# A chain of matmuls and transposes on the output rows, added behind a two-layer block

## The chip, the cores and the metric

The kernel runs on one core of one Trainium2 chip. The time is the device time of one execution in microseconds; before the change its median over two runs is 1359.74 us (1359.56 to 1359.93).

## The reference

The block takes 256 latent tokens and 256 context tokens of 1024 numbers each through two layers and gives back the latent tokens. A layer, cut to what matters:

```python
h = rms_norm(x, norm_w) * (1 + scale) + shift          # scale, shift, gate from c and w_ada
proj = h @ w_in                                        # q, k, v and gate paths of four mixers, merge gates
ys = [windowed, neighbourhood, dense, differential]    # four attentions over latent and context keys
ys = [silu(gate_path) * y for y in ys]
merged = sum(sigmoid(merge_gate[i]) * (ys[i] @ w_br[i]) for i in range(4))
x = x + gate * (merged @ w_out)                        # the second layer's x, latent tokens alone, is the output
```

Everything is float32. What the change adds is in no part of this.

## The kernel before

All weights stream from memory in chunks of 128 x 1024 (`raw`). Each chunk is split exactly into two parts of type fp32r, `wh` and `wl`; so are the activations (`hT`, `yT`, and `gT` and `yT` again for the merged branches). A product is three matmuls, high by high, high by low and low by high (`mm3`), on the full array of 128 rows by 128 columns, with 512, 384 or 256 moving columns. Profiles name the fp32r operands of matmuls `f32`. The one bf16 operand of TensorE is the zero tile of the warm-up: nine matmuls at the start (`WARM`), whose result nobody reads. Transposes are done on TensorE too, 128 x 128 in f32 against the identity `ident`.

The order of the work is not written by hand. The program is recorded first (`Recorder.alt`: each operation with its dependences, found from the parts of the tiles that it reads and writes). Then `schedule` chooses each engine's order by list scheduling: an engine takes the first operation of its list that is ready, TensorE in the order of the recording, the others by the latest start that an earlier schedule gave them (`deadlines`). `search` does this six times, keeps the order whose end by its own model is earliest, and issues that. Matmuls that write one PSUM tile keep their order (`self.chain`). Tiles of one tag share a few slots (`BUFS`: three for `t2k`, two for `t4k`); a tile may be taken ahead of earlier ones of its tag within limits (`RESERVE`, `WINDOW`).

The end of the kernel is `out_proj` of layer 1 (lines 1518 to 1561), with two passes of 512 output columns (`dg`) over two tiles of 128 tokens (`t`). A block's eight times three matmuls fill one PSUM tile; VectorE multiplies it by the gate (`tmp`, tag `t2k`), VectorE or GpSimd adds it to the residual rows `new` (tag `K2`, shown as `K`), and SyncE stores the result to `out`. The very last block, second tile and second pass, goes in two halves of 256 columns. `new[:, 1]` is the second tile of 128 tokens, all 1024 columns; its last quarter is the last thing computed.

In the profile nearly every instruction stands on line 270, the helper that issues the recorded operations; so tiles tell them apart, not lines.

Of the kernel before, what the change touches and what calls it, by code (L numbers as in the profile page):

```python
# [36 lines left out]
# the grid's tokens go column by column, so that 128 of them are half of the grid. Mixer B's keys: one half, the  # L37
# context, the other half; a half's windows reach 8 columns into the other one
# [5 lines left out]
# token-major groups: blocks of 128 columns (mixer, q/k/v/g, index);  # L44
# "S?" is a mixer's gate path and "G??" a merge gate, both feature-major.
# [34 lines left out]
# the adaLN units computed after a group: the next layer's scale and shift, this layer's gate  # L80
# [9 lines left out]
# ---- instruction order: the program is recorded first, then each engine's order is chosen by list  # L90
# scheduling against a model of the engines, and issued in that order ----
ADA = "DPDDGDDGPGGDDGDD"                       # layer 0, shift and scale: units on VectorE (D), GpSimd (G), TensorE (P)
# [8 lines left out]
GATE = 4096 / 1200.0                         # TensorE runs at half its clock after such a time with little work  # L101
# from the end of an instruction to the start of one that needs it; for TensorE with some margin, so that what it
# has in hand covers a late operand
# [10 lines left out]
def _extent(ap):  # L114
    """(partition range, range of elements within a partition's row) that an access pattern touches"""
    dims = ap.ap
    row = dims[0][0]
    n = dims[0][1]
    off = ap.offset
    if row <= 0:  # L120
        return None
    if ap.space == DRAM:
        return 0, 1, min([off] + [off + s * (c - 1) for s, c in dims if s < 0]), 1 + off + sum(
            s * (c - 1) for s, c in dims if s > 0)
    p0, f0 = divmod(off, row)
    lo = hi = f0
    for s, c in dims[1:]:
        if s < 0:
            lo += s * (c - 1)
        else:  # L130
            hi += s * (c - 1)
    return p0, p0 + n, lo, hi + 1


def _run(ap):
    """elements of the contiguous pieces"""
    return ap.ap[-1][1] if ap.ap[-1][0] == 1 else 1
# [13 lines left out]
# PSUM banks are shared by the three uses, each of which is sure of some  # L151
# [22 lines left out]
class Recorder:  # L174
    def __init__(self, nc, pools, plan=None):
# [3 lines left out]
        if plan is not None:                     # tiles are allocated in the order in which the plan uses them  # L179
            self.made = {}  # L180
            for k, slot in plan.slots:
                self.made[k] = self.make(plan.spec[k], slot)
# [3 lines left out]
        self.acc = {}                            # tile name -> [(op, write, extent)]  # L186
        self.tag = {}                            # tile name -> (tag, bufs)
        self.stream = set()                      # tiles of the weights' stream, loaded in order
        self.chain = {}                          # PSUM tile -> its last matmul
# [10 lines left out]
    def tile(self, *spec):  # L200
        """a tile as (pool, shape, type, tag, number of the tag's slots); the plan gives it one of the slots"""
# [13 lines left out]
    # operations that more than one engine can do; the schedule chooses  # L215
# [11 lines left out]
    def alt(self, ways):  # L227
        """one operation, as {engine: (method, args, kw)}"""
# [30 lines left out]
        if "tensor" in ways:                     # accumulation groups of one bank must not interleave  # L259
# [38 lines left out]
    def schedule(self):  # L298
# [6 lines left out]
        # slots: a tile may overtake earlier ones of its tag while a slot is left for those  # L305
# [16 lines left out]
        bank = {}                                # PSUM tile -> {engine: end of its last access}  # L322
        avail = {e: [] for e in ENGS}            # (prio, i) of ops whose producers are all scheduled

        def slot_time(o):
            """time from which the op's tiles have slots, or None"""
# [119 lines left out]
    def deadlines(self):  # L446
        """from a schedule: the latest start of each op at which no instruction of TensorE is late"""
# [20 lines left out]
    def search(self, tries):  # L468
        """the best of several schedules, each with priorities from the deadlines of the one before"""
# [26 lines left out]
class _Builder:  # L496
# [106 lines left out]
    def expand_bias(self, l):  # L603
        """rpbx[h, t, q, i, j] = rpb[h, i + 4, (24 t + j) - (32 t + q) + 15]: column q of half t of the grid,
        rows i of the table that a grid of 4 rows reaches, the 40 columns of keys that the half's windows
        reach; entries outside of a window hold other table entries and are masked later.
        rpbq[h, t, 4 q + r] = rpbx[h, t, q, 3 - r:7 - r]: row r of the grid"""
# [9 lines left out]
    def silu_c(self):  # L617
        """twice silu(c) and silu(c_ctx): as columns, and as rows in every partition"""
# [108 lines left out]
    def split_ops(self, i):  # L727
        """closures that split chunk i, in two halves"""
# [16 lines left out]
    def raw_chunk(self, *key):  # L745
        """the next chunk as it comes"""
# [6 lines left out]
    def chunk(self, *key):  # L753
        """the next chunk, split"""
# [14 lines left out]
    def mm3(self, out, sh, sl, mh, ml, first, last):  # L769
        """stationary (sh + sl) times moving (mh + ml)"""  # L770
# [34 lines left out]
    def ada_unit_pool(self, l, u):  # L805
        """the same on GpSimd, sums on ScalarE"""
# [9 lines left out]
    def ada_unit_pe(self, l, u):  # L816
        """the same on TensorE, as rows that are then transposed"""
# [26 lines left out]
    def norm(self, xt, n):  # L844
        """rows of n token tiles, normalised"""
# [11 lines left out]
    def modulate(self, l, kts, cols, srcs):  # L857
        """h = xn * scale + shift for k tiles kts; srcs: (v, source AP [128, kts, tokens], columns in hf)"""
# [30 lines left out]
    def project_first(self, pre):  # L889
        """the first two groups, chunk by chunk, while h is computed"""  # L890
# [42 lines left out]
    def project_T(self, n, *key):  # L933
        """one block of 128 columns, feature-major"""
# [11 lines left out]
    def sel(self, tab, blocks):  # L946
        """[128, blocks, 64] from a table [128, 2 or 4 mixers, q/k, 64]"""
# [7 lines left out]
    def tabs(self, blocks, t, w):  # L955
        """rotary table w (0 cos, 1 swapped sin) times gain"""
# [5 lines left out]
    def evac_unit(self, u, ps, t, c0, nh):  # L962
        """square sums and raw copy of nh heads of tile t"""
# [12 lines left out]
    def prep_steps(self, u, ts):  # L976
        """norm, gain and rotary of unit u on tiles ts, in place"""
# [34 lines left out]
    def make_q(self, u, blk, tiles):  # L1012
        """[128, 2, tokens]: head 0 as (hi; lo), head 1 as (lo; hi)"""
# [10 lines left out]
    def make_k(self, u, blk):  # L1024
        """[128, hi/lo, 2, 512]: each head's keys in both halves of the partitions"""
# [11 lines left out]
    def evac_v(self, v, ps, t, c0, diff):  # L1037
        """diff: [hi | lo] of 128 columns; else per head [hi | lo] of 64"""
# [10 lines left out]
    def evac_diff_gate(self, g, ps, t):  # L1049
        """token-major gate of mixer D: 2 silu(gate) * subln gain * (1 - lam_init)"""  # L1050
# [13 lines left out]
    def next_bias(self, l, h):  # L1064
        """the bias of head h, loaded one head ahead"""
# [8 lines left out]
    def score_x(self, mix, h, q, j, k, kj, bias, qt, nm):  # L1074
# [9 lines left out]
        elif mix == MIX_B:  # L1084
            near = 32 if qt == 0 else 8          # columns of the grid in front of the context's keys
# [21 lines left out]
    def expo_x(self, S, nm, s, cs=slice(0, 512)):  # L1107
        """numerators, in columns cs of a tile, and their sum"""
# [190 lines left out]
    def split_tiles(self, tag, n):  # L1299
        """room for both parts of [128, n]: one tile if they fit in it"""  # L1300
# [130 lines left out]
    def silu_group(self, l, name):  # L1431
# [3 lines left out]
        per = 512 // n                           # blocks of a tile  # L1435
# [13 lines left out]
    def gate_logits(self, l, m, pr):  # L1449
        """two blocks of 128 output channels of one branch: gate logits"""  # L1450
# [12 lines left out]
    def gate_merge(self, l, m, pr):  # L1463
        """the same blocks: branch projection, gate, merge"""
# [33 lines left out]
    def store_gates(self, l):  # L1498
        """the gate's columns as rows in memory"""
# [9 lines left out]
    def load_gates(self, l, v):  # L1509
        """the gate in every partition: [128 (any token), 1024]"""  # L1510
# [7 lines left out]
    def out_proj(self, l, v, mT, src, finish):  # L1518
# [14 lines left out]
        for dg in range(2):  # L1533
            # (tokens, columns, sum); the last block in halves: one is finished while the other is computed
# [50 lines left out]
    def build(self):  # L1585
# [27 lines left out]
        for l in range(DEPTH):  # L1613
# [41 lines left out]
            else:  # L1655
                self.out_proj(l, 0, mT, self.xmid, a["out"])


class _Unit:
    """up to two blocks of 128 q/k columns of one mixer, over the token tiles"""  # L1660

    def __init__(self, blocks):
# [3 lines left out]
        self.ready = 0                           # tiles whose q/k are prepared  # L1666


def _rows(w):
    """[K, N] -> [K/256, 128, 2 * N]: rows in chunks of 256"""  # L1670
# [3 lines left out]
def _blocks(w, nb):  # L1674
    """[K, N] -> [N / (128 nb), 128, nb * K]: columns in nb blocks of 128, all rows"""
# [5 lines left out]
def _tokens():  # L1681
    """where in the sequence the tokens come from"""
# [4 lines left out]
def _shape_constants():  # L1687
# [6 lines left out]
    # indexed by where the factor comes from: what lands in half 0 is negated  # L1694
# [61 lines left out]
```

## Time and profile before

| | |
|---|---|
| median of the two runs | 1359.74 us (1359.56 to 1359.93) |
| span of the profiled execution | 1355.9 us; its own time is given as this span alone |
| what lies around the span, against the median | 3.8 us |
| TensorE (PE) busy | 1266.3 us, 93% of the span, 7286 matmuls |
| VectorE (DVE) busy | 1094.4 us, 81% |
| ScalarE (ACT), GpSimd (POOL) busy | 741.8 us (55%), 696.1 us (51%) |
| mean granted TensorE clock | 0.981 of 2.4 GHz |

The span runs from the first to the last instruction of one execution; the time of a run is a little longer. A matmul is shown with the time from its start to its end, and the next starts before that end; the pace of a row of matmuls is therefore read from their starts, not from their durations. PEld is the loading of the stationary operand, which goes on beside the matmuls. The granted clock is 1.00 at 2.4 GHz and 0.50 at 1.2 GHz.

### The profile page before, as it was taken

Reading aid. Unit: us, or ns where it says so; the run is one execution under the profiler, and the core shown is the slowest. Engines: PE = TensorE matmul, PEld = TensorE weight load, DVE = VectorE, ACT = ScalarE, POOL = GpSimd, SP = SyncE. Lnnn points to the kernel's source line nnn. Section 1 sums busy time; section 2 is a strip of 40 time slices with the busy share of each in tenths; the row PEclk is TensorE's granted clock in tenths of the full one; section 3 lists DMA queues with packets and bytes.
Section 4 is the critical chain, followed back from the end, with each engine's and each line's share of the span. In section 5 each row is a group of like instructions: output and inputs, shape, how many; then the busy total and the mean of one; then the engine's idle time right before and its main releaser. Section 6 shows DMA issues by size and latency. Waiting matters only on the chain. (4 is left out here: it accounts for less than half of the span.)

```text
span 1355.9 us, 21375 instructions
## 1 busy us (share of the span) xinstructions
PE 1266.3 (93%) x7286; PEld 1086.5 (80%) x7286; DVE 1094.4 (81%) x2108; ACT 741.8 (55%) x1738; POOL 696.1 (51%) x694
## 2 busy tenths in 40 slices
PE   7688999999999999999999999899999899899998
PEld 5466778789877989778777887888889899788897
DVE  7999974974998688995788568798995878886877
ACT  6466843463765346633456345577664556554563
POOL 4784224424554655534364236665754756475643
PEclk8899999999999999999999999999999999999999
DMA  6531133313322432243322266231436534343454
GB/s 244 179 123 42 47 105 98 124 58 114 90 87 94 147 114 72 88 153 100 105 63 78 85 208 203 81 125 51 138 114 176 166 121 140 100 127 105 143 168 172
DMA packets 64576, 160.90 MB, mean 119 GB/s; under 512 B 13482, under 2 KB 24914, under 8 KB 64468
## 3 DMA queue, kind: packets, MB, share of 16 engines
q1 hardware_dynamic: 64468, 159.55, 37.3%
q8 instruction: 57, 0.93, 0.3%
q14 instruction: 51, 0.42, 0.1%
HBM read 157.42 MB, written 5.88 MB: 120 GB/s over the span
## 5 line engine op out<-in xcount | busy, mean ns | idle before, releaser
L270 POOL TENSOR_TENSOR wl<-raw,wh 128x512 fp32r<-128x512 f32 (+2 forms) x233 | 307.6, 1324 | 341.0 <-PE ppj L270 179.6
L270 PE MATMUL ppj<-wh,hT 128*128 128x512 f32 (+2 forms) x1424 | 388.2, 351 | 18.5 <-DVE hT L270 14.2
L270 ACT ACTIVATE wh<-raw 128x512 fp32r<-128x512 f32 (+2 forms) x394 | 233.3, 600 | 250.7 <-PE ppj L270 187.9
L270 PE MATMUL ppj<-hT,wh 128*128 128x512 f32 (+1 forms) x1408 | 368.5, 345 | 0.0
L270 PEld LDWEIGHTS ppj<-wh,hT 128*128 128x128 f32 x1424 | 253.5, 192 | 45.1 <-DVE hT L270 16.8
L270 PEld LDWEIGHTS ppj<-hT,wh 128*128 128x128 f32 x1408 | 244.0, 191 | 27.4 <-ACT t2k L270 0.2
L270 DVE TENSOR_TENSOR wl<-raw,wh 128x512 fp32r<-128x512 f32 (+2 forms) x247 | 199.5, 817 | 77.9 <-PE ppj L270 63.3
L270 PE MATMUL ppj<-wl,hT 128*128 128x512 f32 (+2 forms) x712 | 248.3, 349 | 1.2 <-DVE wl L270 0.7
L270 PE MATMUL ppj<-hT,wl 128*128 128x512 f32 (+1 forms) x704 | 242.9, 345 | 1.8 <-DVE wl L270 1.8
L270 PEld LDWEIGHTS ppj<-wl,hT 128*128 128x128 f32 x712 | 136.8, 192 | 14.8 <-POOL wl L270 1.6
L270 ACT ACTIVATE P<-psc,st 128x512 f32<-128x512 f32 (+2 forms) x192 | 114.8, 601 | 60.8 <-DVE st L270 53.3
L270 PEld LDWEIGHTS ppj<-hT,wl 128*128 128x128 f32 x704 | 134.4, 191 | 16.0 <-DVE wl L270 2.5
L270 PE MATMUL ppj<-yT,wh 128*128 128x512 f32 (+1 forms) x512 | 131.7, 341 | 0.4 <-DVE yT L270 0.4
L270 PE MATMUL psc<-K,Q 128*128 128x512 f32 (+2 forms) x384 | 99.1, 367 | 13.8 <-DVE Q L270 8.4
L270 PE MATMUL ptr<-ident,P 128*128 128x128 f32 x560 | 88.1, 277 | 17.4 <-DVE P L270 12.5
L270 DVE TENSOR_REDUCE st<-psc 128x1 f32<-128x512 f32 (+2 forms) x160 | 102.3, 660 | 1.0
L270 POOL TENSOR_TENSOR st<-st,expo 128x8 f32<-128x8 f32 (+3 forms) x68 | 97.5, 1437 | 2.5
L270 PEld LDWEIGHTS ppj<-yT,wh 128*128 128x128 f32 x512 | 87.5, 189 | 10.6 <-DVE yT L270 0.8
L270 PEld LDWEIGHTS ptr<-ident,P 128*128 128x128 f32 x560 | 64.9, 141 | 37.6 <-DVE P L270 10.3
L270 PEld LDWEIGHTS psc<-K,Q 128*128 128x128 f32 x384 | 63.6, 192 | 33.2 <-DVE Q L270 12.0
L270 PE MATMUL ptr<-t4k,V 128*128 128x256 f32 x480 | 78.4, 289 | 11.1 <-DVE t4k L270 9.0
L270 PE MATMUL ppj<-yT,wl 128*128 128x512 f32 (+1 forms) x256 | 86.8, 339 | 1.0 <-DVE wl L270 1.0
(176 smaller groups left out, 2139.2 us busy)
## 6 DMA issues: line engine op xcount, KB each, us to landing
raw<-in_w_G SPq DMA_DIRECT2D x64, 512.0 KB
raw<-in_w_ada SPq DMA_DIRECT2D x43, 512.0 KB
raw<-in_w_br SPq DMA_DIRECT2D x32, 512.0 KB
raw<-in_w_in_D SPq DMA_DIRECT2D x32, 512.0 KB
raw<-in_w_S SPq DMA_DIRECT2D x24, 512.0 KB
raw<-in_w_in_B SPq DMA_DIRECT2D x32, 384.0 KB
raw<-in_w_out SPq DMA_DIRECT2D x24, 512.0 KB
raw<-in_w_in_A SPq DMA_DIRECT2D x8, 512.0 KB
```

The lines of the kernel that those rows point to most:

```text
L270: getattr(getattr(self.nc, eng), fn)(*args, **kw)
```

## The change

`out_proj` of the last layer hands its rows back, and a new method, `strokes`, records work on the second tile of them. VectorE makes four copies: `z` (1024 columns, fp32r), `b` (1024 columns, bf16), `y` (512 columns, f32) and `one` (the identity, fp32r). On these, TensorE does 124 matmuls and transposes, each a group by itself (`start` and `stop` set), into four PSUM tiles that nothing reads:

- 12 fp32r and 12 bf16 matmuls of 512 columns on all 128 rows, and 8 fp32r ones whose columns come in two pieces of 256;
- 12 fp32r and 12 bf16 ones of 128 columns;
- 20 fp32r ones of 512 columns on 64 rows, in turn on the lower and the upper half of the partitions and into two PSUM tiles, then 8 on the lower half alone;
- 6 times such a pair and two matmuls on all rows;
- 8 f32 transposes of 128 x 128, and 8 in fp32r.

The stationary operand has 128 columns in all of them. `LO` and `HI` are partitions 0 to 63 and 64 to 127. Apart from this the diff takes comments and docstrings away.

```diff
             else:
-                self.out_proj(l, 0, mT, self.xmid, a["out"])
+                new = self.out_proj(l, 0, mT, self.xmid, a["out"])
+                self.strokes(new)
...
+    def strokes(self, new):
+        nc = self.nc
+        z = self.t([128, 2, 512], "t4k", F32R)
+        nc.vector.tensor_copy(z.rearrange("p a b -> p (a b)"), new[:, 1])
+        b = self.t([128, 2, 512], "t2k", BF16)
+        nc.vector.tensor_copy(b.rearrange("p a b -> p (a b)"), new[:, 1])
+        y = self.t([128, 512], "t2k")
+        nc.vector.tensor_copy(y, new[:, 1, 0:512])
+        one = self.t([128, 128], "t2k", F32R)
+        nc.vector.tensor_copy(one, self.ident)
+        ps = [self.pt([128, 512], "pj") for _ in range(4)]
+        mm = lambda o, w, x: nc.tensor.matmul(o, w, x, start=True, stop=True)
+        for _ in range(12):
+            mm(ps[0], z[:, 0, 0:128], z[:, 1])
+        for _ in range(12):
+            mm(ps[1], b[:, 0, 0:128], b[:, 1])
+        for _ in range(8):
+            mm(ps[2], z[:, 0, 0:128], z[:, :, 0:256])
+        for _ in range(12):
+            mm(ps[3][:, 0:128], z[:, 0, 0:128], z[:, 1, 0:128])
+        for _ in range(12):
+            mm(ps[0][:, 0:128], b[:, 0, 0:128], b[:, 1, 0:128])
+        for _ in range(10):
+            for h, q in ((0, LO), (1, HI)):
+                mm(ps[1 + h], z[q, 0, 0:128], z[q, 1])
+        for _ in range(8):
+            mm(ps[0], z[LO, 0, 0:128], z[LO, 1])
+        for _ in range(6):
+            for h, q in ((0, LO), (1, HI)):
+                mm(ps[1 + h], z[q, 0, 0:128], z[q, 1])
+            for k in (0, 3):
+                mm(ps[k], z[:, 0, 0:128], z[:, 1])
+        for k in range(8):
+            c = slice(k % 4 * 128, k % 4 * 128 + 128)
+            nc.tensor.transpose(ps[0][:, c], y[:, c], self.ident)
+        for k in range(8):
+            c = slice(k % 4 * 128, k % 4 * 128 + 128)
+            nc.tensor.transpose(ps[1][:, c].bitcast(F32R), z[:, 0, c], one)
```

## Rows read from the trace of the kernel before

**Rows 1.** The page: its first line, and TensorE's granted clock in 40 equal slices, in tenths.

```profile
span 1355.9 us, 21375 instructions
...
PEclk8899999999999999999999999999999999999999
```

**Rows 2.** The chain of waits from 1340 on, its end: start, us, what.

```profile
1351.66 0.64 issue
1352.30 0.76 POOLq L1737
```

**Rows 3.** The timeline at the end: start, us, engine, operation, count, idle time before.

```profile
1351.52 0.28 PE L270 MATMUL ppj<-wh,yT 128*128 128x256 f32 x1
1351.69 1.73 SPq L270 DMA_DIRECT2D out_dram<-K  x2
1351.84 0.42 DVE L270 TENSOR_TENSOR t2k<-ppj,t4k 128x256 f32<-128x256 f32 x1 [1.00 <-PE ppj L270]
1352.34 0.72 POOL L270 TENSOR_TENSOR K<-K,t2k 128x256 f32<-128x256 f32 x1 [0.68 <-DVE t2k L270]
```

**Rows 4.** Waits of SyncE from 1330 on: us in total, times, longest.

```profile
SPq L1737 <- DMA out_dram<-K: 1.3, 1, 1.3
SPq L1737 <- PEq L1737: 0.6, 2, 0.4
```

**Rows 5.** The timeline at the start: a cast, and the weight load that waits for it.

```profile
4.61 0.68 DVE L270 CAST V<-t4k 2x1024 fp32r<-2x1024 f32 x1
...
5.34 0.18 PEld L270 LDWEIGHTS psc<-V,st 2*128 2x128 f32 x1 [1.06 <-DVE V L270]
```

**Rows 6.** The timeline of 512-column matmuls: the first and the last of 25.

```profile
1334.61 0.40 PE L270 MATMUL ppj<-wh,gT 128*128 128x512 f32 x1
...
1340.18 0.39 PE L270 MATMUL ppj<-wh,yT 128*128 128x512 f32 x1
```

**Rows 7.** The warm-up: two weight loads of the timeline, four apart; its matmuls grouped by form.

```profile
2.42 0.15 PEld L270 LDWEIGHTS <-t2k 128*128 128x128 bf16 x1 [0.28 <-issue]
...
4.13 0.15 PEld L270 LDWEIGHTS <-t2k 128*128 128x128 bf16 x1 [0.28 <-issue]
...
L270 PE MATMUL ppj<-t2k 128*128 128x512 bf16 x9 | 4.0, 626 | 1.2 <-DVE expo L270 1.2
```

**Rows 8.** The timeline of 256-column matmuls: the first (the last is in rows 3).

```profile
1349.37 0.40 PE L270 MATMUL ppj<-wh,yT 128*128 128x256 f32 x2
```

**Rows 9.** Transposes: four in the timeline; all grouped by form (busy us, mean ns).

```profile
706.42 0.60 PE L270 MATMUL ptr<-ident,P 128*128 128x128 f32 x4
...
L270 PE MATMUL ptr<-ident,P 128*128 128x128 f32 x560 | 88.1, 277 | 17.4 <-DVE P L270 12.5 <-DVE st L270 2.8 <-ACT P L270 0.8
```

**Rows 10.** Matmuls on 2 rows in the timeline, two steps apart.

```profile
5.68 0.39 PE L270 MATMUL ptr<-V,st 2*128 2x512 f32 x1
...
6.15 0.39 PE L270 MATMUL ptr<-V,st 2*128 2x512 f32 x1
```

**Rows 11.** Two idle times in the timeline, and the stretch after each.

```profile
1259.97 0.39 PE L270 MATMUL ppj<-hT,wl 128*128 128x256 f32 x1 [1.77 <-DVE wl L270]
...
1261.08:1264.49 3.41, 2.84 (x14) 2.54 (x14) 3.41 (x10) 1.94 (x8) 1.59 (x3) 0.50 0.75 246
...
1057.38 0.63 PE L270 MATMUL ptr<-ident,P 128*128 128x128 f32 x4 [1.83 <-DVE P L270]
...
1056.28:1059.69 3.41, 2.31 (x19) 2.19 (x20) 3.41 (x9) 2.67 (x8) 3.33 (x5) 1.00 0.04 17
```

**Rows 12.** Stretches: us, PE, PEld, DVE, ACT, POOL busy (count), clock, DMA share, GB/s.

```profile
4.97:8.39 3.42, 2.58 (x10) 1.34 (x9) 3.13 (x6) 1.75 (x5) 0.42 (x2) 1.00 1.04 422
8.39:11.80 3.41, 2.43 (x11) 2.01 (x12) 2.50 (x6) 2.54 (x5) 1.72 (x3) 0.50 1.02 412
...
561.35:564.76 3.41, 1.99 (x9) 1.63 (x10) 3.25 (x6) 1.78 (x3) 1.20 (x1) 1.00 0.80 205
564.76:568.17 3.41, 3.41 (x19) 2.78 (x19) 3.27 (x8) 0.90 (x4) 0.00 (x0) 1.00 0.26 102
```

## Prediction

> **What bounds the kernel now.** I read the page first: the span is 1355.9 us, and TensorE's clock stands at nine tenths or more of full speed in all but the first two slices [rows 1]. The two timed runs have a median of 1359.74 us, so 3.8 us lie around the span; I add the change to the span and carry those 3.8 us along unchanged. The change is appended, so the rest is about the last microseconds. The chain of waits, read at its end, shows the reader that TensorE no longer decides there: behind its last work come an addition on GpSimd and then GpSimd's closing instruction [rows 2]. The timeline gives the times: the last matmul starts at 1351.52 and ends at 1351.80; VectorE's product runs to 1352.26; GpSimd adds it to the output rows from 1352.34 to 1353.06; the store that this releases is issued by 1353.42 [rows 3]. SyncE then waits 1.3 us for it to land [rows 4], that is to about 1354.8. What is left to 1355.9, about 1.1 us, is the closing of the program, in which SyncE waits for TensorE's sequencer too [rows 4].
>
> **The change, part by part.** The 124 matmuls and transposes read copies of the second 128 output rows, and the copy takes both halves of their columns, so it waits for that last addition at 1353.06. No earlier work is there to run them beside. They are on the path to the end all the same, though nobody reads them: the closing waits for TensorE's sequencer [rows 4].
>
> *Start.* The first twelve need the copy z, 1024 elements per partition from f32 to fp32r on VectorE. Such a cast took 0.68 us, and TensorE took it over about 0.05 us after it ended, 5.34 against 5.29 [rows 5]. With 0.03 us to get from GpSimd to VectorE, as the store's issue had it [rows 3], TensorE starts at 1353.06 + 0.03 + 0.68 + 0.05 = 1353.82. The copies to bf16 (as long), of 512 elements (half) and of the identity follow on VectorE in some 1.3 us while TensorE works through its first twelve (2.8 us); without that cover the bf16 twelve would start at most 0.7 us late. The memory for the copies is the one that the last products leave, and the last of those is done before any copy of the rows can start, so no slot is waited for.
>
> *fp32r, 512 columns, all rows: 12 + 8, and 12 of the mixed stretch.* From 1334.61 to 1340.18 there are 24 steps from start to start: 0.232 us each [rows 6]. The eight that read their columns in two pieces are taken alike, since the pieces are contiguous. 12 x 0.232 = 2.78, 8 x 0.232 = 1.86.
>
> *bf16, 512 columns: 12.* The warm-up's bf16 matmuls came 0.428 us apart, (4.13 - 2.42) / 4 [rows 7]. That is 512 columns at 1.2 GHz, so I take half, 0.214: 2.57 us; the upper end is the fp32r step, 2.78.
>
> *128 columns: 12 fp32r, 12 bf16.* Not in the trace. Upper end: the 256-column step, 18 steps from 1349.37 to 1351.52, so 0.119 [rows 3, 8], should the weights' load set it. Lower end: a quarter of the 512-column step, 0.058 for fp32r and 0.054 for bf16. For fp32r I take the nearest row, the transposes of 128 columns with a weight load each: four in 0.60 us of which one lasts 0.28, so (0.60 - 0.28) / 3 = 0.107 [rows 9]: 1.28 us. For bf16, whose weight load of 0.15 us in the warm-up is shorter than fp32r's 0.18 [rows 5, 7], the middle, 0.086: 1.03 us.
>
> *64 rows: 20 in alternating halves of the partitions, 8 on the lower half, 12 in the mixed stretch.* No matmul before uses 64 rows. The nearest is one of 2 rows and 512 columns: (6.15 - 5.68) / 2 = 0.235 us a step [rows 10], the same as with all rows, so few rows alone save nothing. A pair on different halves lies between one step (0.232) and two (0.464). Every row that I have follows one at a time, so I take two: 20 x 0.232 = 4.64, 8 x 0.232 = 1.86, and the mixed stretch 24 x 0.232 = 5.57. Twelve times the number of rows changes between 64 and 128. A matmul lasts 0.40 and the next starts after 0.232 [rows 6]; if each change had to wait for the end of the one before, that would be 12 x 0.17 = 2.0 us. I take nothing, since no row shows such a wait, and keep the 2.0 for the range.
>
> The Trainium skill, page "TensorEngine Tiling", section "Tiling Modes", says that going from one tiling mode to another drains TensorE; by that the 2.0 us would be paid, and the sum would be higher by that much. No run before shows it.
>
> *Transposes: 8 f32, 8 fp32r.* f32: 8 x 0.107 = 0.86 [rows 9]. For fp32r, the same, with 0.058 as lower end (0.46).
>
> *Sum.* 2.78 + 2.57 + 1.86 + 1.28 + 1.03 + 4.64 + 1.86 + 5.57 + 0.86 + 0.86 = 23.3 us of TensorE; it starts the last one by 1377.1 and finishes it 0.17 us past its step, at 1377.3. With 1.1 us of closing the span ends at 1378.4, against 1355.9: **+22.5 us, 1382.2 us**. The store's landing, which ended the kernel before, is over at 1354.8 and costs nothing more.
>
> *Clock.* TensorE idles from 1351.80 to 1353.82, 2.0 us. The trace has it both ways: after an idle time of 1.77 us the next stretch was granted 0.50, after one of 1.83 us it stayed at 1.00 [rows 11]. Such a drop lasted 3.4 us, in which matmuls take twice as long: 1.7 us lost. I take none, the longer of the two gaps being nearer, and keep 1.7 for the range.
>
> **Rivals.** A: the halves run side by side. Against it: nothing in the trace ever overlapped. For it: the diff gives the two halves different banks of PSUM, as independent work needs. Then 10 + 6 pairs save a step each, 16 x 0.232 = 3.7 us: 1378.5 us, up to 1380.5 with the 2.0 us of changes.
>
> The Trainium skill, page "TensorE: Matmul & The Clock Gate", Part 3, says just this: matmuls whose operands start at different row groups run concurrently. The trace has none to test it.
>
> B, beyond 2%: the clock falls in the stretch of 64-row work and stays low. In the trace ten matmuls, eight of them on 2 rows, were followed by a stretch at 0.50, while nine on all rows kept 1.00 [rows 12]; so few rows seem to count as less work, and 64 lies between 2 and 128. Price: from the first of the 20 on, 52 matmuls at 0.428 instead of 0.232, 10.2 us: 1392.4 us. "Slower by over 2%" (about what a measurement of this kernel can tell from no change) begins at 1386.9, so it decides once 24 of them run at the lower clock. Against it: half the rows, back to back, should still be more work than a stretch with long idle times that kept the clock.
>
> C: nothing is added that the end has to wait for: about 1360 us. Against it: the warm-up's nine matmuls, which nobody reads either, are in the trace [rows 7].
>
> D: the order of the kernel is planned anew from the longer record and another order comes out for the work before. All new work but the identity's copy depends on the last rows, so I see no reason for it; it could go either way by tens of us, as TensorE idles about 90 us in all.
>
> **How the numbers follow.** The forecast, one by one, has 0.45; A 0.35; B 0.11; C 0.03; D 0.06, in thirds over faster, within and slower. Faster by over 2%: 0.02. Slower: 0.11 + 0.02 = 0.13. Within: 0.85. Predicted: 1382 us. Low end: A with 128-column matmuls and fp32r transposes at their lower ends (0.6 + 0.4 + 0.4 = 1.4 us less): 1377. High end: the forecast with 128-column and bf16 matmuls at their upper ends (0.7), a drop of the clock at the start (1.7) and the changes of rows (2.0): 1386.6, so 1387. Left out are B, C and most of D, 0.19.
>
> **What would show it.** In the profile after, the last addition on GpSimd should stand near 1353, the first new matmul 0.8 us behind it, and the span end about 1 us after the last transpose. Two matmuls on different halves starting together instead of 0.23 us apart show A; a granted clock of 0.50 from the twenty on shows B, one at the very start the drop. A wait in the mixed stretch at each change of rows shows the 2.0 us. If the work before 1351 has moved, it is D. The prediction is wrong if the new matmuls last over 28 us, or if the end doesn't wait for them.

## The result, and the profile after

The changed kernel takes 1378.62 us (1378.49 to 1378.75, two runs) against 1359.74: the ratio is 1.0138, 95% interval [1.0119, 1.0157]. The predicted 1382 us is 3.4 us too high, inside the range of 1377 to 1387, and the time stays within 2%. Timed again beside the experiments it was 1380.76 us, ratio 1.0165 [1.0144, 1.0186].

The timeline of the changed kernel at the point where [rows 3] stop, with the columns of that group:

```profile
1352.01 0.28 PE L270 MATMUL ppj<-wh,yT 128*128 128x256 f32 x1
...
1352.90 0.72 POOL L270 TENSOR_TENSOR K<-K,t2k 128x256 f32<-128x256 f32 x1 [0.67 <-DVE t2k L270]
1353.66 0.69 DVE L270 CAST t4k<-K 128x1024 fp32r<-128x1024 f32 x1 [0.84 <-POOL K L270]
1354.27 0.68 DVE L270 CAST t2k<-K 128x1024 bf16<-128x1024 f32 x1
1354.41 0.50 PE L270 MATMUL ppj<-t4k 128*128 128x512 f32 x1 [2.12 <-DVE t4k L270]
```

The last addition ends at 1353.62, the cast begins 0.04 us later, and TensorE starts 0.79 us behind the addition. The old work ends 0.49 us later than before; in other executions with the chain its last matmul started as early as 1350.12 or as late as 1353.41, so that is scatter.

The end of the chain of waits, and SyncE's waits. The landing of a store and 0.6 us for TensorE's sequencer [rows 4] are still among the waits; the one of 20.5 us is new:

```profile
1354.36 0.04 issue
1354.41 21.60 PE ppj L270 x123
```

```profile
SPq L1779 <- PE ppj L270: 20.5, 1, 20.5
...
SPq L1779 <- DMA out_dram<-K: 1.3, 1, 1.3
```

The store has landed, and the program waits 20.5 us more, for nothing but TensorE. The chain by its parts (stretch, its length, PE busy with count, granted clock, DMA share and GB/s; a count takes in matmuls that reach into a stretch):

```profile
1354.40:1357.26 2.86, 2.85 (x12) 1.00 0.16 52
1357.26:1359.87 2.61, 2.61 (x14) 1.00 0.00 0
1359.87:1361.72 1.85, 1.85 (x9) 1.00 0.00 0
1361.72:1363.01 1.29, 1.29 (x13) 1.00 0.00 0
1363.01:1363.79 0.78, 0.78 (x14) 1.00 0.00 0
1363.79:1366.17 2.38, 2.38 (x22) 1.00 0.00 0
1366.17:1367.98 1.81, 1.81 (x11) 1.00 0.00 0
1367.98:1374.32 6.34, 6.34 (x24) 1.00 0.00 0
1374.32:1375.11 0.79, 0.79 (x9) 1.00 0.00 0
1375.11:1376.01 0.90, 0.89 (x11) 1.00 0.00 0
```

| part | predicted us | measured us |
|---|---|---|
| 12 fp32r, 12 bf16, 8 fp32r in two pieces, 512 columns | 2.78, 2.57, 1.86 | 2.86, 2.61, 1.85 |
| 12 fp32r, 12 bf16, 128 columns | 1.28, 1.03 | 1.29, 0.78 |
| 20 on 64 rows, halves in turn | 4.64 | **2.38** |
| 8 on the lower half | 1.86 | 1.81 |
| mixed stretch, 24 | 5.57 | **6.34** |
| 16 transposes, to the last one's end | 1.89 | 1.69 |

The reader is to see the sixth stretch: twenty matmuls in the time of ten. The timeline has the last bf16 ones and the first eight of the twenty, which are over in 1.20 us, where eight one after another at 0.227 would need 7 x 0.227 + 0.39 = 1.98:

```profile
1363.31 0.55 PE L270 MATMUL ppj<-t2k 128*128 128x128 bf16 x7
1363.79 1.20 PE L270 MATMUL ppj<-t4k 64*128 64x512 f32 x8
```

The twenty's starts lie in pairs, the two of a pair 0.003 to 0.017 us apart. And the mixed stretch, where pairs share a time too, is longer, not shorter, than 24 steps. The weight loads show where the time goes: a block of two loads begins only 0.24 to 0.37 us after the one before it has ended, while in the row of eight on the lower half 0.04 us lie between loads. What holds a block back the profile doesn't name (`issue`):

```profile
1368.30 0.30 PEld L270 LDWEIGHTS ppj<-t4k 128*128 128x128 f32 x2 [0.35 <-issue]
1368.96 0.19 PEld L270 LDWEIGHTS ppj<-t4k 64*128 64x128 f32 x2 [0.37 <-issue]
1369.40 0.30 PEld L270 LDWEIGHTS ppj<-t4k 128*128 128x128 f32 x2 [0.24 <-issue]
1370.06 0.18 PEld L270 LDWEIGHTS ppj<-t4k 64*128 64x128 f32 x2 [0.37 <-issue]
```

A round takes 1.10 us (1368.30 to 1369.40) for a pair and two full matmuls, three steps of 0.227, so 0.42 us more than the steps: 0.2 us for each of its two changes of rows.

### The profile page after: what moved, and what is told of

It is laid out like the page before. It is cut to its first block, busy times and chain, and to the rows that moved or that the text cites. A ratio compares the mean times of both kernels' runs of the same rounds, so it can differ in the third digit from the quotient of the medians.

```text
span 1376.9 us, 21629 instructions
## 1 busy us (share of the span) xinstructions
PE 1288.7 (94%) x7410; PEld 1102.4 (80%) x7410; DVE 1094.3 (79%) x2112; ACT 741.0 (54%) x1738; POOL 699.2 (51%) x694
## 5 line engine op out<-in xcount | busy, mean ns | idle before, releaser
L270 DVE TENSOR_TENSOR wl<-raw,wh 128x512 fp32r<-128x512 f32 (+2 forms) x247 | 194.9, 799 | 77.4 <-PE ppj L270 62.6
```

The lines of the kernel that those rows point to most:

```text
L270: getattr(getattr(self.nc, eng), fn)(*args, **kw)
```

## The experiments

Theory 1: matmuls on different halves of the partitions run at once, and a change between 64 and 128 rows costs about 0.2 us. The rivals: two PSUM tiles are what lets two run at once; the alternation of tiles, or the pairs, cost the time of the mixed stretch; and, for the total, that part of the chain is hidden or is there only under the profiler. None of these kernels touches the output rows, only the work behind them.

**The same kernel once more.**

> The changed kernel once more, timed beside the others. Its first profile grew by 21.0 us of span, its first two times by 18.9 us. If the chain lies wholly behind the old end, time and span grow alike: about 21 us, 1380 to 1381 us. If part of the growth exists only under the profiler, the time stays 18 to 19 us above the kernel before.

Four times, 1378.17 to 1384.94 us, ratio 1.0165: the median is 22.0 us above the kernel before in the same series (19.6 to 25.3 by the interval), and 1380.76 lies in the 1380 to 1381 expected. Each execution's time was about 2.0 us above its span (1378.59 and 1376.6), and the kernel before stood 2.1 to 2.2 us above its own in the same series (1357.27 and 1355.1): the growth is no matter of the profiler. The profile also showed what the first had not, a fall of the clock at the start, behind the same idle time of 2.12 us. Its timeline, and the stretch (busy PE, PEld, DVE, ACT, POOL, then the clock):

```profile
1352.52 4.61 PE L270 MATMUL ppj<-t4k 128*128 128x512 f32 x12 [2.12 <-DVE t4k L270]
1356.97 2.76 PE L270 MATMUL ppj<-t2k 128*128 128x512 bf16 x12
```

```profile
1353.20:1356.60 3.40, 3.40 (x10) 2.61 (x9) 0.00 (x0) 0.00 (x0) 0.00 (x0) 0.50 0.03 5
```

The first twelve took 4.45 us (1352.52 to 1356.97) instead of 2.86: 1.6 us lost. Of eight profiles with the chain, five show this fall and three don't.

**The chain twice.**

```diff
-        for _ in range(12):
-            mm(ps[0], z[:, 0, 0:128], z[:, 1])
...
+        for _ in range(2):
+            for _ in range(12):
+                mm(ps[0], z[:, 0, 0:128], z[:, 1])
...
```

> The chain of 124 is recorded twice. If all of it lies on the path to the end at the pace of the profile, one more chain costs 21.4 us (its TensorE time, 1354.41 to 1375.84) over the changed kernel in time as in span: about 1400 us. If a part of a chain is hidden, or the clock falls on the way, the second one costs another amount: 19 us or less, or 25 us and more.

```profile
1354.46:1377.48 23.02, 23.02 (x124) 0.93 0.02 6
1377.48:1398.90 21.42, 21.42 (x126) 1.00 0.00 1
```

The second chain took 21.42 us, the first 1.6 more, with a mean clock of 0.93: it had the fall at the start. The time was 1399.22 us, ratio to the kernel before 1.0299 [1.0284, 1.0314], so 38.6 to 42.7 us for two chains; the 21.0 us of the first profile and these 21.4 make 42.4. Between the two medians, though, lie only 18.5 us (1399.22 and 1380.76), which by the words of the expectation would mean a hidden part. The executions of each kernel scatter by 5 to 7 us, so the medians can't decide between 18.5 and 21.4; the trace does: the second chain follows the first without a pause and takes 21.42 us, all of it behind the old work. No part of the chain is hidden.

**All twenty on the lower half.**

```diff
         for _ in range(10):
-            for h, q in ((0, LO), (1, HI)):
-                mm(ps[1 + h], z[q, 0, 0:128], z[q, 1])
+            for h in (1, 3):
+                mm(ps[h], z[LO, 0, 0:128], z[LO, 1])
```

> The twenty 64-row matmuls all read the lower half of the partitions, still in turn into two PSUM tiles. Theory 1 (different halves of the partitions run at once): they come one at a time, 20 x 0.227 = 4.5 us instead of 2.4, the kernel 2.1 us longer than the changed one. Theory 2 (two PSUM tiles are what lets two matmuls run at once): they stay at 2.4 us and the time stays.

```profile
1366.78:1371.44 4.66, 4.66 (x22) 3.79 (x21) 0.00 (x0) 0.00 (x0) 0.00 (x0) 1.00 0.00 0
```

4.66 us instead of 2.38, still with two PSUM tiles in turn: the halves of the partitions make the difference. The time, 1384.05 us against 1380.76, has the sign of the 2.3 us, but the intervals of the two ratios overlap ([1.0154, 1.0194] here); the verdict rests on the trace. Different halves into one and the same PSUM tile were not run, so whether the two tiles are needed as well isn't shown.

**Mixed stretch, grouped.**

```diff
         for _ in range(6):
             for h, q in ((0, LO), (1, HI)):
                 mm(ps[1 + h], z[q, 0, 0:128], z[q, 1])
+        for _ in range(6):
             for k in (0, 3):
                 mm(ps[k], z[:, 0, 0:128], z[:, 1])
```

> The mixed stretch in another order: first the six pairs on 64 rows, then the twelve matmuls on 128 rows in their alternation of two tiles, so one change of rows instead of eleven within it. Theory 1 (each change between 64 and 128 rows costs about 0.2 us): it falls from 6.3 us to 6 x 0.227 + 12 x 0.23 + 0.2 to 0.4 = 4.4 us, the kernel 2 us shorter. Rival (alternating PSUM tiles or the pairs themselves cost the extra time): it stays near 6.3 us.

```profile
1366.46:1370.77 4.31, 4.31 (x24) 3.24 (x21) 0.00 (x0) 0.00 (x0) 0.00 (x0) 1.00 0.00 0
```

```profile
1362.27 5.29 PEld L270 LDWEIGHTS ppj<-t4k 64*128 64x128 f32 x40
1367.91 2.59 PEld L270 LDWEIGHTS ppj<-t4k 128*128 128x128 f32 x12 [0.35 <-issue]
```

4.31 us instead of 6.34, with the same matmuls into the same tiles and one wait of the loads left instead of eleven: 2.03 / 10 = 0.20 us for each change taken away. Time 1377.17 us, 3.6 below the unchanged chain in the same series, with overlapping intervals of the two ratios again ([1.0121, 1.0150] here). The trace accounts for 2.0 of it; what the rest is isn't shown.

**One and one.**

```diff
-        for _ in range(6):
-            for h, q in ((0, LO), (1, HI)):
-                mm(ps[1 + h], z[q, 0, 0:128], z[q, 1])
-            for k in (0, 3):
-                mm(ps[k], z[:, 0, 0:128], z[:, 1])
+        for _ in range(12):
+            mm(ps[1], z[LO, 0, 0:128], z[LO, 1])
+            mm(ps[0], z[:, 0, 0:128], z[:, 1])
```

> The mixed stretch replaced by twelve times one matmul on the lower 64 rows and one on 128 rows: 24 matmuls, 23 changes of rows inside, no pairs. Theory 1 (about 0.2 us per change): 24 x 0.227 + 23 x 0.2 = 10 us instead of 6.3. Rival (the extra time belongs to the pairs): 24 x 0.227 = 5.4 us.

```profile
1372.22 0.18 PEld L270 LDWEIGHTS ppj<-t4k 64*128 64x128 f32 x1 [0.24 <-issue]
1372.65 0.19 PEld L270 LDWEIGHTS ppj<-t4k 128*128 128x128 f32 x1 [0.25 <-issue]
1373.09 0.18 PEld L270 LDWEIGHTS ppj<-t4k 64*128 64x128 f32 x1 [0.25 <-issue]
...
1377.30 0.29 PEld L270 LDWEIGHTS ppj<-t4k 128*128 128x128 f32 x1 [0.44 <-issue]
1378.02 0.28 PEld L270 LDWEIGHTS ppj<-t4k 64*128 64x128 f32 x1 [0.44 <-issue]
```

```profile
1372.97:1376.40 3.43, 3.43 (x9) 1.48 (x8) 0.00 (x0) 0.00 (x0) 0.00 (x0) 1.00 0.00 0
1376.40:1379.80 3.40, 3.40 (x6) 1.43 (x5) 0.00 (x0) 0.00 (x0) 0.00 (x0) 0.50 0.00 0
```

At full clock a step is 0.43 us (1372.22 to 1373.09 is two): 0.227 plus 0.20, without any pair. So the cost belongs to the change of rows. This kernel was executed once (1389.32 us). Then came what nobody had expected of this run: after 5.5 us of this the clock fell to 0.50, a step became 0.72 us, and the 24 took 13.1 us, not 10. So a fall like rival B's exists, here behind 64 and 128 rows in turn with a wait at each change; which of the two brought it isn't shown.

**Copies alone.** The 124 matmuls and transposes are left out.

```diff
         mm = lambda o, w, x: nc.tensor.matmul(o, w, x, start=True, stop=True)
+        return
```

> The four copies on VectorE alone, without the 124 matmuls and transposes. In the changed kernel the last copy ended 1.3 us behind the last addition, while the store's landing is awaited until 1.8 us behind it. So if the chain on TensorE is the whole cost: no difference from the kernel before, at most 0.3 us. If the copies cost (by their place before the last products, or by a lengthened end): 0.5 to 1.5 us more.

1358.65 us against 1357.93, ratio 1.0004 [0.9992, 1.0016]: no difference that the times can tell, between 1.1 us less and 2.2 more. That alone would not rule out the 0.5 to 1.5 us for the copies; the trace does:

```profile
1354.47 0.72 POOL L270 TENSOR_TENSOR K<-K,t2k 128x256 f32<-128x256 f32 x1 [0.68 <-DVE t2k L270]
```

The addition ends at 1355.19 and the span at 1358.0, 2.8 us later, as before the change (1353.06 and 1355.9): the copies behind the rows lengthen nothing. And the last 500 matmuls of the old work take 69.53 us from the first one's start to the last one's, here as before the change: the copies that went ahead did not delay TensorE there. TensorE's chain is the cost.

**Few rows for long.**

```diff
+        for k, q in ((0, LO), (3, slice(0, 32)), (3, slice(0, 2))):
+            for _ in range(60):
+                mm(ps[k], z[q, 0, 0:128], z[q, 1])
```

> Behind the chain, 60 matmuls of 512 columns on the lower 64 rows, 60 on 32 rows and 60 on 2 rows, one at a time. Rival B of the prediction (few rows count as little work for the clock): the granted clock falls to 0.50 in the stretch of 64 rows, or in that of 32 or 2, and the step goes from 0.227 to 0.427 us. If only the columns count: 1.00 throughout, three times 13.6 us. The stretch at the start with 2 rows before a fall speaks for a fall with 2 rows at least; for 64 rows I expect none.

```profile
1377.73:1391.57 13.84, 13.84 (x61) 10.97 (x60) 0.00 (x0) 0.00 (x0) 0.00 (x0) 1.00 0.01 1
1393.00:1416.19 23.19, 23.19 (x55) 17.65 (x55) 0.00 (x0) 0.00 (x0) 0.00 (x0) 0.50 0.00 0
1416.19:1441.70 25.51, 25.51 (x61) 19.23 (x59) 0.00 (x0) 0.00 (x0) 0.00 (x0) 0.50 0.00 1
```

```profile
1391.57:1393.00 1.43, 1.43 (x7) 0.98 0.00 0
```

Sixty matmuls on 64 rows, back to back, kept 1.00 for 13.8 us. With 32 rows, just as dense, the clock fell 1.4 us into the stretch (the last line, with PE's columns alone) and stayed at 0.50, and with 2 rows it did not come back. So B's reason is borne out, fewer rows were followed by a fall where more were not, but not for the 64 rows of this chain. This is one execution (1444.94 us) with the three stretches in one order; other orders were not run.

**Twenty in blocks.**

```diff
-        for _ in range(10):
-            for h, q in ((0, LO), (1, HI)):
+        for h, q in ((0, LO), (1, HI)):
+            for _ in range(10):
                 mm(ps[1 + h], z[q, 0, 0:128], z[q, 1])
```

> The twenty 64-row matmuls as ten on the lower half and then ten on the upper half. If TensorE starts matmuls strictly in program order, the first upper one starts with the tenth lower one or behind it, and the twenty take 19 to 20 steps of 0.227, 4.3 to 4.5 us. In the changed kernel one upper matmul seems to start 0.67 us ahead of the lower one before it in the program, so I expect the upper block to start about three steps early: 3.6 to 3.9 us. If it may pass freely, 2.4 us.

```profile
1362.55:1363.68 1.13, 1.13 (x6) 1.00 0.00 0
1363.68:1364.48 0.80, 0.80 (x8) 1.00 0.00 0
1364.50:1365.18 0.68, 0.68 (x6) 1.00 0.00 0
1365.18:1366.00 0.82, 0.82 (x9) 1.00 0.00 0
```

The second and the fourth stretch are the dense ones. The records don't name the half; but twenty on the lower half alone came 0.23 us apart (4.66 us), so a second row of starts in between can only be the upper half's. The first upper matmul starts at 1363.69, beside the seventh of the ten lower ones, so three ahead of its place; from 1364.49 the upper ones run alone until 1365.19, when the eight lower ones behind them in the program begin, again three early. The twenty took 3.9 us (1362.21 to 1366.1), within the 3.6 to 3.9 expected, in one execution (1378.12 us). TensorE does not start matmuls strictly in program order, but it passes only three here.

## Why the prediction was right, and where it was not

*Place and closing.* Right: start 0.79 us behind the addition (0.76 predicted), everything behind it on TensorE, no wait for the copies, 0.9 us of closing (1.1). The double chain and the copies alone show that nothing is hidden and that nothing else costs. One reading was off, without harm: the piece `POOLq L1737` [rows 2], taken for GpSimd's closing, covers the time of the last addition [rows 3], and in the changed kernel the same piece (1352.87 to 1353.64) stands ahead of the first cast.

*Paces.* Those read from starts held: fp32r of 512 columns 0.23 us [rows 6], f32 transposes 0.11 [rows 9], a few rows no faster than many [rows 10]. The 128-column fp32r took the transposes' 0.107. The bf16 ones, put in the middle at 0.086, came at their lower end of 0.054: about 0.056 from start to start (seven of them took 0.55 us, of which the last one lasts 0.22); their 0.78 us hold some 0.1 us of the change to 64 rows that follows. fp32r transposes, 0.085 from start to start, lie below f32's 0.109.

*Halves.* The step that failed: "Every row that I have follows one at a time, so I take two." Two run at once; the twenty took 2.38 us, not 4.64. That was rival A, to which I gave 0.35, by the rule of the Trainium skill, page "TensorE: Matmul & The Clock Gate", Part 3. The trace now agrees: starts 0.003 to 0.017 us apart. The rows before could not say so, having no matmul on an upper half. My reason against it, that nothing in the trace overlapped, was no reason.

*Changes of rows.* "I take nothing, since no row shows such a wait, and keep the 2.0 for the range." It was 0.20 a change against the bound's 0.17, some 2.3 us over twelve. In the mixed stretch it ate all that the six pairs saved there, 1.4 us, and 0.8 more. The Trainium skill, page "TensorEngine Tiling", section "Tiling Modes", says that a change of mode drains TensorE; the trace agrees as far as each change costs 0.20 us. That the two omissions cancelled in part, -2.3 and +0.8, was luck.

*Clock.* The sum took no fall at the start, and the first profile had none; five of eight had one, 1.6 us against the 1.7 of the bound. Two idle times of nearly the same length, with different outcomes [rows 11], had said that it may go either way. B did not occur: the stretch on 64 rows kept 1.00, unlike what followed the one on 2 rows [rows 12].

*Sum.* TensorE 21.6 us instead of 23.5 (the 23.3 and the last one's 0.17): -2.3 halves, +0.8 changes, -0.2 bf16, -0.2 transposes, +0.1 the first matmuls, rounded. Closing -0.2, the old work +0.5: 21.0 us of span against 22.5. The other 1.9 of the 3.4 us came with "those 3.8 us": the time less the span is 1.8 to 2.2 in all executions that list both, and 2.1 to 2.2 for the kernel before, so the profiled execution was faster than the median by some 1.6 us (an estimate, as its own time is not on record), and I added its span's growth to the slower pair. That rival A's 1378.5 us all but equals the measured time is luck too: with the changes paid A stood at 1380.5, and about 2 us too much lay in the 3.8.

*Order.* The sentence that all new work but the identity's copy depends on the last rows was wrong: the 512 columns of the f32 copy are done earlier, and it moved ahead of the last products. It took 1.41 us (from 1343.99 on), not half of 0.68. It cost nothing, as the copies alone show. D did not occur: TensorE's 7286 earlier matmuls come in the same sequence of shapes and tiles as before in every profile here.

## What to carry to other kernels

Work behind the last output cost its whole length here, though nobody reads it. On TensorE, contractions of 64 rows gained only where neighbours in the program used different halves of the partitions (here always with different PSUM tiles too), and they lost 0.2 us each time the number of rows changed; so group them by rows and alternate the halves. Price a tail with the clock that an idle time in front of it may cost: behind the same 2.1 us idle the clock fell in five executions of eight, which cost 1.6 us.

## What the runs showed of the hardware

- A matmul on the free half started up to three places ahead of its turn in the program (the twenty in blocks).
- At 512 columns without a pause, TensorE stayed at 2.4 GHz through 13.8 us on 64 rows and fell to 1.2 GHz 1.4 us into the 32 rows that followed (one execution). It fell too after 5.5 us of one matmul on 64 rows and one on 128 in turn, each with its 0.2 us of waiting (one execution).
- bf16 matmuls of 128 columns came 0.056 us apart with a weight load each, fp32r ones 0.11 (1.29 us for twelve).
